# One-hot products with wide moving tokens, token tiles refilled when free, read-backs in turn, splits ahead of additions

## The chip, the cores and the metric

The kernel runs on one core of one Trainium2 chip. The metric is the device time of one execution in microseconds (us); times of the kernel before are the median of three runs. TensorE (PE) multiplies 128-row tiles, VectorE (DVE), ScalarE (ACT) and GpSimd (POOL) work on tiles of 128 partitions, SyncE (SP) issues most of the DMAs, and 16 DMA engines move the data between DRAM and the on-chip buffers. Each engine takes its instructions in the order in which the program holds them.

## The reference

512 tokens of 1024 values pass through one encoder layer: a norm, a mixer of a state-space branch and a latent attention, a cross-attention into 256 memory tokens, and a mixture of experts; everything in float32. The change lies in the mixture of experts, which is, for the 512 x 1024 matrix `t` of normed rows:

```python
g_idx = argmax(softmax(t @ w_group + b_group))            # one of 4 groups
top_v, top_i = top_k(e_logits of that group, 2)           # 2 of its 8 experts
gates = softmax(top_v) * max(g_prob), placed at the two experts, 0 elsewhere
for each of 32 experts e:
    out += (silu(t @ w_gate[e]) * (t @ w_up[e]) * gates[:, e]) @ w_down[e]
x = x + out;  result = rms(x) * norm_final_g
```

`w_gate` and `w_up` are 32 x 1024 x 256, `w_down` is 32 x 256 x 1024: 3 MB for each expert, 96 MB in all, and every expert's weights are read once.

## The kernel before

**The work before the experts.** Up to about 460 us of the span the kernel computes the mixer and the cross-attention. The last part of that, the output projection of the cross-attention (`pxo`), adds its result to the rows `X[t]`, t = 0 to 3, four tiles of 128 tokens. The four lie in two buffers (`xr`, two token tiles in each). The rows are written to two DRAM tables as they come: `hd`, from which they are gathered later, and `xd`, to which results are added.

**Routing.** For every token tile, `choose(t)` (L1385 on) takes the two experts on VectorE, and `place(t)` (L1423 on) has TensorE count, for each token and expert, how many tokens came before it (`prank`). A comparison of that rank with 64 slot numbers gives, for experts 0 and 1, a one-hot matrix `oh0[:, t]` of 128 tokens x 128 places (2 experts of 64 places). The experts are worked on in 16 pairs, with 64 places for each expert, so that a pair is a tile of 128 rows. `codes(t)` makes the one-hot tiles for the look-up of pairs 0 and 1, for three of the four token tiles on GpSimd and ScalarE, with `XG[1]` as the scratch. The list `OQ` (L64) is the written order of these steps: `00` is the one-hot product of token tile 0 and half 0, `P2` is `choose` and `place` of tile 2, `C0` is `codes(0)`.

**The first pair's rows.** Pair 0 isn't gathered: its rows are made by TensorE, straight in transposed form. `one_hot_T(g, c)` (L1439) takes, for half c of the 1024 values, four slices of 128 values of `X[t]` as weights (128 x 128) and the one-hot matrix (128 columns) as the moving operand, and sums over the four token tiles in a bank `px0[c]`. That is 4 x 2 x 4 = 32 products. `evac_T` (L1416) then multiplies a bank by the norm's gain into `XT`. All these products are tied in order to each other by `behind`, which fixes the order of issue without a wait.

**Look-up and gathers.** After the last one-hot product, `look_up` (L1591, `ptab0`) finds the token of each place, and `tokens` (L1602) writes the indices `IX`. With them GpSimd gathers the rows of pair n from `hd` into `XG[n % 2]` (L1694). Both `XG` tiles are first cleared, `XG[1]` at L1584 and `XG[0]` at L1699, because places without a token are skipped by a gather.

**The expert loop.** For pair n, `first(n)` transposes the gathered rows (`get`, L1764, eight transposes), multiplies by the gate and up weights (`pG`, L1784) and gates the result. `second(n)` (L1821 on) transposes it and multiplies by the down weights (`pD`, L1841). In pair 0, `get(1, 0)` stands between the first six and the last two slices of k. In iteration n, `second(n - 1)` follows `first(n)`. The results of pairs 0 to 13 are scattered into `xd` and `yd` (L1855), a token's first expert to one and its second to the other. Those of pairs 14 and 15 are split into a high and a low part (`split`, on ScalarE and VectorE) and are added at the end by products with a one-hot matrix (`last_sum`, L1915).

**The loads.** SyncE issues the expert weights in a fixed order, 96 tiles of 1 MB (`order`), into 24 buffers (`ring` and `tags`), most of which were used for other things earlier. `load_to(n)` (L1297) issues up to the n-th tile. A tile is issued when its buffer is free, and SyncE waits at a tile whose buffer isn't. The last two tiles of the first 24 (tag `X`, tiles 22 and 23) lie where `xr` was. For them alone (`after`, L1303) GpSimd writes a few zeros into the new tile, in an order behind the first gather, and the loads wait for that write. The call that reaches them, `load_to(ahead)`, is at L1700. Tiles 24 and 25 take the buffers of pair 0's first two weight tiles, 26 and 27 those of its other two.

**The end.** After the last scatter `take_back` (L1861) reads `yd` and then `xd` back, four reads of 512 KB each. VectorE's order at the end is written out by `turn_`. `both(t)` adds the two tables of token tile t. `down15` is the second half of pair 15 with its two splits, one for each half of the columns. Before, the order is split 0, `both(0)`, split 1, `both(1)`, `both(2)`, `both(3)`, then the additions of the sums (`a00` and on, the list `TO`). The rows of token tiles 2 and 3 are added on TensorE by products with the identity (L1909), those of tiles 0 and 1 by VectorE (L1924). Squares on ScalarE, a reciprocal and a product on VectorE and a store follow for each token tile and half.

## Time and profile before

| | |
|---|---|
| median of 3 runs | 732.78 us (732.72 to 732.96) |
| the profiled execution's own time | 733.54 us |
| its span, first to last instruction | 731.4 us |
| PE busy | 682.5 us (93%) |
| DVE busy | 416.3 us (57%) |
| ACT busy | 248.7 us (34%) |
| POOL busy | 113.8 us (16%) |
| chain that ended last | PE 52%, DMA 28%, DVE 13% of the span |
| granted TensorE clock, mean | 0.978 |

A row of a timeline gives the start in us from the first instruction of the span, the length, the engine, the line of the kernel, the operation, and output<-input. In brackets stands how long the engine was idle before it, and what ended that idle time. PEld is TensorE's load of weights, which runs beside its products. A product in float32 appears as two instructions, so the 32 one-hot products are 64 rows. A tile that is renamed in the source appears under the name of its first use: `px0` is shown as `pX`, the token tiles as `xr`. DMA share is the mean busy share of the 16 DMA engines.

### The profile page before, as it was taken

How to read it: one execution, taken by the hardware profiler on the slowest of the kernel's cores; microseconds unless marked ns; L12 is line 12 of the kernel's file. 1: busy time of each engine (PE TensorE's matmuls, PEld its weight loads, DVE VectorE, ACT ScalarE, POOL GpSimd, SP SyncE). 2: the span in 40 equal slices, each digit the busy share in tenths (PEclk: the TensorE clock that was granted, in tenths of full speed). 3: DMA queues.
4: the chain of work that ended last, by engine and by line, in shares of the span. 5: the costliest groups of instructions: out<-in, count | busy, mean ns of one | idle time of the engine just before them, and what ended most of it. 6: DMA issues, size and time to landing. Idle time of an engine off the chain costs nothing.

```text
span 731.4 us, 10262 instructions
## 1 busy us (share of the span) xinstructions
PE 682.5 (93%) x3684; PEld 469.9 (64%) x3684; DVE 416.3 (57%) x975; ACT 248.7 (34%) x511; POOL 113.8 (16%) x172
## 2 busy tenths in 40 slices
PE   5998988987999999999999999999998999998875
PEld 4696877975878887888878788963333333433333
DVE  4799997957477887555466543552533421221127
ACT  5642354344565766334345422221101000000023
POOL 6300002003300001102000001212332232232100
PEclk9999999999999999999999999999999999999996
DMA  7773132435452254232328896869999999999983
GB/s 213 168 206 109 38 74 67 114 123 127 145 164 68 92 153 131 99 84 84 107 80 339 271 338 240 282 251 390 409 408 408 410 404 410 407 413 388 397 337 121
DMA packets 102013, 165.84 MB, mean 227 GB/s; under 512 B 32762, under 2 KB 64606, under 8 KB 98120
## 3 DMA queue, kind: packets, MB, share of 16 engines
q1 hardware_dynamic: 95512, 157.58, 61.0%
q0 software_dynamic: 6432, 7.58, 3.1%
q8 instruction: 30, 0.49, 0.3%
q14 instruction: 23, 0.19, 0.1%
q10 hardware_dynamic: 16, 0.00, 0.0%
HBM read 154.59 MB, written 25.69 MB: 246 GB/s over the span
## 4 chain that ended last, share of the span: by engine, by line
PE 52%; DMA 28%; DVE 13%; ACT 2%; issue 2%; SPq 1%; POOL 0%; DVEq 0%; ACTq 0%
DMA gu<-moe_w_up 15%; DMA dn<-moe_w_down 6%; PE pG L1784 3%; DVE lo L214 2%; PE po L1034 2%; DMA raw<-w_in 2%; PE pX L1443 2%; PE pxq L268 2%; PE pxq L266 2%; PE pxq L267 2%; DMA gu<-moe_w_gate 2%; PE pD L1841 2%; PE pxo L266 2%; PE pPT L1023 2%; PE pxo L267 2%
## 5 line engine op out<-in xcount | busy, mean ns | idle before, releaser
L1784 PE MATMUL pG<-gu,XT 128*64 128x512 f32 x512 | 126.7, 595 | 5.3 <-DMA gu<-moe_w_up 5.2
L214 DVE TENSOR_TENSOR lo<-raw,hi 128x1024 fp32r<-128x1024 f32 (+3 forms) x64 | 75.9, 1190 | 60.5 <-ACT hi L204 60.1
L204 ACT ACTIVATE hi<-raw 128x1024 fp32r<-128x1024 f32 (+3 forms) x64 | 63.9, 1002 | 102.0 <-issue 21.1
L1784 PEld LDWEIGHTS pG<-gu,XT 128*64 128x64 f32 x512 | 40.4, 136 | 71.8 <-issue 68.5
L1841 PE MATMUL pD<-dn,aT 128*64 128x512 f32 x256 | 73.2, 601 | 1.8 <-DMA dn<-moe_w_down 1.8
L1807 DVE SCALAR_TENSOR_TENSOR a<-pG,RS,sl 128x256 f32<-128x256 f32 x16 | 10.7, 670 | 105.8 <-ACT sl L1801 65.4
L1801 ACT ACTIVATE sl<-pG,RS 128x256 f32<-128x256 f32 x16 | 7.6, 474 | 131.9 <-PE pG L1784 131.9
L1841 PEld LDWEIGHTS pD<-dn,aT 128*64 128x64 f32 x256 | 20.5, 136 | 36.4 <-issue 31.6
L1417 DVE TENSOR_TENSOR XT<-pX,gmo 128x512 f32<-128x512 f32 x32 | 22.0, 686 | 20.9 <-PE pX L1768 16.8
L1803 POOL TENSOR_SCALAR YY<-XG,F 128x1024 f32<-128x1024 f32 x13 | 15.2, 1169 | 107.1 <-issue 46.9
L1768 PEld LDWEIGHTS pX<-ident,XG 128*128 128x128 f32 x120 | 15.7, 194 | 25.0 <-issue 17.2
L1849 DVE SCALAR_TENSOR_TENSOR YY<-pD,GT,YY 128x512 f32<-128x512 f32 x26 | 19.5, 749 | 21.1 <-PE pD L1841 21.0
L1827 ACT ACTIVATE aT<-pA 128x256 f32<-128x256 f32 x16 | 6.1, 384 | 61.4 <-PE pD L1841 46.0
L1768 PE MATMUL pX<-ident,XG 128*128 128x128 f32 x120 | 21.0, 298 | 5.3 <-DMA XG<-hd,IX 5.2
L267 PE MATMUL pxq<-gT,hi 128*128 128x512 f32 x64 | 25.6, 400 | 0.0
L266 PE MATMUL pxq<-gT,hi 128*128 128x512 f32 x64 | 25.5, 399 | 0.0
L268 PE MATMUL pxq<-gT,lo 128*128 128x512 f32 x64 | 25.4, 396 | 0.0
L266 PE MATMUL pcq<-hT,hi 128*128 128x512 f32 x48 | 20.0, 416 | 2.8 <-DVE s_t L593 2.8
L267 PE MATMUL pq<-lo,cq 128*128 128x384 f32 x48 | 18.1, 376 | 2.3 <-DVE lo L214 2.3
L268 PE MATMUL pcq<-hT,lo 128*128 128x512 f32 x48 | 19.7, 410 | 0.0
L267 PE MATMUL pcq<-hT,hi 128*128 128x512 f32 x48 | 19.5, 407 | 0.0
L1855 POOL DMA_INDIRECT xd<-YY,IY x14 | 14.7, 1047 | 30.7 <-DVE YY L1849 25.7
(617 smaller groups left out, 1690.0 us busy)
## 6 DMA issues: line engine op xcount, KB each, us to landing
gu<-moe_w_gate SPq DMA_DIRECT2D x64, 512.0 KB
gu<-moe_w_up SPq DMA_DIRECT2D x64, 512.0 KB
dn<-moe_w_down SPq DMA_DIRECT2D x30, 1024.0 KB
raw<-w_in SPq DMA_DIRECT2D x9, 512.0 KB
raw<-xattn_w_v SPq DMA_DIRECT2D x8, 512.0 KB
raw<-xattn_w_k SPq DMA_DIRECT2D x8, 512.0 KB
raw<-w_out SPq DMA_DIRECT2D x8, 512.0 KB
raw<-xattn_w_q SPq DMA_DIRECT2D x8, 512.0 KB
```

What stands on the lines that cost most here:

```text
L204: anchor["act"] = nc.scalar.activation(hi, r, AF.Copy)
L214: anchor["dve"] = nc.vector.tensor_tensor(lo, r, hi.bitcast(F32), OP.subtract)
L266: i = nc.tensor.matmul(o, lh, rh, start=start, stop=False)
L267: nc.tensor.matmul(o, lh, rl, start=False, stop=False)
L268: anchor["pe"] = nc.tensor.matmul(o, ll, rh, start=False, stop=stop)
L1417: return v.tensor_tensor(xt, ps.rearrange("p (k t) -> p k t", k=4), gmo[:, 4 * c:4 * c + 4, None].to_broadcast([128, 4, 128]), OP.mult)
L1768: i = nc.tensor.transpose(ps[:, k * 128:k * 128 + 128], xg[:, 4 * c + k], ident)
L1784: i = nc.tensor.matmul(pg[64 * s:64 * s + 64], xt[c][:, kk, 64 * s:64 * s + 64], ew[2 * n + s, c][:, :, kk], start=k == 0, stop=k == 7)
L1803: nc.gpsimd.tensor_scalar(result(n), XG[n % 2], F1[:, n:n + 1], 1.0, OP.mult, OP.mult)
L1841: i = nc.tensor.matmul(pd[64 * s:64 * s + 64], at_[:, f, 64 * s:64 * s + 64], ew[2 * n + s, 2][:, f, c * 512:c * 512 + 512], start=f == 0, ...
L1849: yield v.scalar_tensor_tensor(o, pd, GT[:, n:n + 1], o, OP.mult, OP.add)
L1855: nc.gpsimd.indirect_dma_start(out=o, out_offset=bass.IndirectOffsetOnAxis(ap=IY[:, w, n:n + 1], axis=0), in_=Y, in_offset=None, bounds_ch ...
```

## The change

Four things are altered.

1. `one_hot_T` becomes `one_hot`: the one-hot matrix is the weight operand and 512 values of the token rows move, in one product for a token tile and a half, 8 in all. The rows come out untransposed. Two copies, one on ScalarE and one on VectorE, bring them into `XG[0]`, TensorE transposes them in eight steps and `evac_T` follows as before. The clearing of `XG[0]` goes. The token look-up keeps its place behind all of this in TensorE's order.
2. The loads of tiles 22 and 23 lose GpSimd's write and with it their place behind the first gather.
3. `take_back` reads `yd` and `xd` of one token tile after each other, into one buffer.
4. Both splits of pair 15 come ahead of all `both` additions. Besides, the transposes of pair n are put behind the last `pD` product of pair n - 2 in TensorE's order.

```diff
-            after = nheld + 1 + NF < nld[0] <= ahead
...
-                if after:
-                    behind(nc.gpsimd.memset(t[0:1, :, 0, 0:1], 0.0), gat[-1])
...
-    def one_hot_T(g, c):
+    def one_hot(g, c):
 
         for t in range(GR[g].start, GR[g].stop):
-            for k in range(4):
-                i = nc.tensor.matmul(px0[c][:, k * 128:k * 128 + 128],
-                                     X[t].rearrange("t (p k) -> t k p", k=8)[:, 4 * c + k],
-                                     oh0[:, t].rearrange("p e s -> p (e s)"), start=t == 0 and k == 0,
-                                     stop=t == NT - 1 and k == 3)
-                behind(i, last[0])
-                last[0] = i
+            i = nc.tensor.matmul(px0[c], oh0[:, t].rearrange("p e s -> p (e s)"), X[t][:, c * 512:c * 512 + 512],
+                                 start=t == 0, stop=t == NT - 1)
+            behind(i, last[0])
+            last[0] = i
...
-            one_hot_T(g, c)
-            if g == len(GR) - 1:
-                evac_T(xt0[c], px0[c], c)
-    gz = nc.gpsimd.memset(XG[1], 0.0)
+            one_hot(g, c)
+    nc.scalar.activation(XG[0][:, 0:512], px0[0], AF.Copy)
+    nc.vector.tensor_copy(XG[0][:, 512:D], px0[1])
+    for c in range(2):
+        ps = bankt(f"pXt0{c}")
+        for k in range(4):
+            i = nc.tensor.transpose(ps[:, k * 128:k * 128 + 128],
+                                    XG[0].rearrange("t (p k) -> t k p", k=8)[:, 4 * c + k], ident)
+            behind(i, last[0])
+            last[0] = i
+        evac_T(xt0[c], ps, c)
+    nc.gpsimd.memset(XG[1], 0.0)
...
-    nc.gpsimd.memset(XG[0], 0.0)
...
             behind(i, last[0])
+            behind(i, lastd.get(n - 2))
...
+            lastd[n] = i
...
-        for src, dst in ((yd, back), (xd, X)):
-            for t in range(NT):
-                if t % 2 == 0:
-                    xb = slot(next(free), [128, 2, D], f"xb{t}")
-                nc.sync.dma_start(xb[:, t % 2], src[128 * t:128 * t + 128])
-                dst[t] = xb[:, t % 2]
+        for t in range(NT):
+            xb = slot(next(free), [128, 2, D], f"xb{t}")
+            for i, (src, dst) in enumerate(((yd, back), (xd, X))):
+                nc.sync.dma_start(xb[:, i], src[128 * t:128 * t + 128])
+                dst[t] = xb[:, i]
...
-    for t, i in enumerate(down15):
+    for i in down15:
         turn_("v", i)
-        both(t)
-    for t in on_pe:
+    for t in range(NT):
         both(t)
```

## Rows read from the trace of the kernel before

**Rows 1.** The page, part 2: what the DMA engines moved in each fortieth of the span (18.3 us each), in GB/s.

```profile
GB/s 213 168 206 109 38 74 67 114 123 127 145 164 68 92 153 131 99 84 84 107 80 339 271 338 240 282 251 390 409 408 408 410 404 410 407 413 388 397 337 121
```

**Rows 2.** The chain of work that ended last, in order of time, from 530 us: start, length, and what ran or was waited for.

```profile
530.02 14.48 DMA gu<-moe_w_gate
...
699.36 1.93 PE pD L1841 x6
701.51 9.72 DMA xb<-xd
...
713.29 4.63 PE pC L1915 x10
717.93 2.52 PE pC L1909 x4
...
721.38 1.72 PE pC L1909 x4
```

**Rows 3.** Busy time by stretch (all engines): length, PE, PEld, DVE, ACT, POOL busy with their counts, granted clock, DMA share, GB/s.

```profile
480.00:485.00 5.00, 4.86 (x35) 3.35 (x34) 2.82 (x6) 0.00 (x0) 1.18 (x2) 1.00 0.14 57
485.00:490.00 5.00, 4.74 (x37) 1.69 (x34) 4.16 (x36) 1.62 (x4) 1.83 (x4) 1.00 0.67 229
490.00:495.00 5.00, 5.00 (x26) 2.13 (x26) 2.98 (x6) 0.64 (x2) 0.00 (x0) 1.00 1.00 310
495.00:500.00 5.00, 5.00 (x26) 1.60 (x24) 0.00 (x0) 0.00 (x0) 0.00 (x0) 1.00 0.99 382
...
550.00:600.00 50.00, 45.74 (x224) 17.12 (x221) 18.49 (x51) 3.51 (x10) 14.81 (x14) 1.00 1.02 406
```

**Rows 4.** The SyncE queue's waits between 460 and 500 us: waiting line, what it waited for, total, times, longest.

```profile
SPq L1308 <- POOL gu L1307: 14.9, 1, 14.9
```

**Rows 5.** Timeline of 480 to 500 us, the DMA issues only: the first gather by GpSimd and the loads that SyncE issues after it.

```profile
484.36 1.35 POOL L1694 DMA_INDIRECT XG<-hd,IX  x1 [3.82 <-DVE IX L1605]
...
485.83 0.33 SPq L1308 DMA_DIRECT2D gu<-moe_w_gate  x1
...
487.87 0.39 SPq L1308 DMA_DIRECT2D gu<-moe_w_gate  x1
...
492.99 0.91 SPq L1323 DMA_DIRECT2D dn<-moe_w_down  x2
```

**Rows 6.** The chain again, 465 to 493 us: the pieces of the one-hot products (L1443), and of the second pair's transposes (L1768) and the first pair's last products (L1784).

```profile
465.54 1.02 PE pX L1443 x4
...
467.00 1.91 PE pX L1443 x8
...
469.73 2.93 PE pX L1443 x12
472.72 3.90 PE pX L1443 x16
476.71 5.82 PE pX L1443 x24
...
490.46 0.64 PE pX L1768 x4
491.10 1.87 PE pG L1784 x8
```

**Rows 7.** Timeline of 463 to 480 us: the routing of the last token tile (its logits, the places of the tile before, its own places), ScalarE's code operations and the clearing that follows them.

```profile
469.83 0.25 DVE L1391 SCALAR_TENSOR_TENSOR r_lg<-plog,st_moe,br 128x36 f32<-128x36 f32 x1 [2.39 <-PE plog L1362]
...
472.77 0.29 DVE L1435 TENSOR_TENSOR oh<-prank,slots 128x128 f32<-128x128 f32 x1 [1.28 <-PE prank L1430]
...
476.76 0.29 DVE L1435 TENSOR_TENSOR oh<-prank,slots 128x128 f32<-128x128 f32 x1 [1.57 <-PE prank L1430]
...
477.18 0.71 ACT L1562 ACTIVATE XG<-XG 128x256 f32<-128x256 f32 x2
...
479.59 0.95 POOL L1584 MEMSET XG<- 128x1024 f32 x1 [4.72 <-ACT ohb L1563]
```

**Rows 8.** Timeline of 480 to 500 us: an evacuation of transposed rows, the token look-up, the first expert product, the token indices.

```profile
480.65 0.69 DVE L1417 TENSOR_TENSOR XT<-pX,gmo 128x512 f32<-128x512 f32 x1 [2.91 <-PE pX L1443]
...
482.35 0.34 PE L1595 MATMUL ptab<-vals,ohb 128*128 128x2 bf16 x8
...
482.63 1.93 PE L1784 MATMUL pG<-gu,XT 128*64 128x512 f32 x6
...
483.35 0.17 DVE L1605 TENSOR_SCALAR IX<-TK 128x2 int32<-128x2 f32 x1
```

**Rows 9.** The gathered tile XG: time from issue to landing of its 15 gathers.

```profile
DMA to landing us min/median/max: 7.0/8.4/8.9
```

**Rows 10.** Timeline of the last 47 us: ScalarE's half of the last split, the additions of the read-back tables, the additions of the sums, the last squares.

```profile
707.01 0.69 ACT L276 ACTIVATE Y<-pD,GT 128x512 fp32r<-128x512 f32 x1 [1.03 <-PE pD L1841]
711.35 1.23 DVE L1939 TENSOR_TENSOR xb<-xb,xb 128x1024 f32<-128x1024 f32 x1 [4.58 <-DMA xb<-xd]
...
713.15 3.49 DVE L1939 TENSOR_TENSOR xb<-xb,xb 128x1024 f32<-128x1024 f32 x3
...
716.56 2.47 DVE L1924 TENSOR_TENSOR xb<-xb,pC 128x512 f32<-128x512 f32 x4
...
723.59 0.60 ACT L329 ACTIVATE fin<-pC 128x512 f32<-128x512 f32 x1 [0.82 <-PE pC L1915]
```

**Rows 11.** Busy time by stretch near the end (columns as in rows 3).

```profile
714.00:715.00 1.00, 1.00 (x4) 0.81 (x3) 1.00 (x2) 0.00 (x0) 0.00 (x0) 0.50 0.06 25
```

More of the change, by code (lines that the diff above doesn't have):

```diff
@@ L1311, in load_to @@
                 t = slot(tag, [128, 2, D], f"dn{e}")
-                if after:
-                    behind(nc.gpsimd.memset(t[0:1, 0, 0:1], 0.0), gat[-1])
                 if i == 94:
@@ L1751, in overflow @@
                     nc.sync.dma_start(out[0, t * 128:t * 128 + 128, half[c]], o[:, t])
-    silu, YY = [None], []
+    silu, YY, lastd = [None], [], {}
     turns = {}
```

## The prediction

> **What bounds the kernel now.** I read the page's bandwidth line first: from about 494 us to 696 us the DMA engines move close to 410 GB/s, and before that they don't [rows 1]. The chain of waits says the same from its side: from 530 us on it consists of weight loads, up to the last down products at 699.36, and then of the read-back of the tables and the closing sums [rows 2]. So the second half is a stream of weights at full rate, and its end is set by when the stream was first able to run without a gap. The stretches show the gap: the share is 0.14 between 480 and 485 us and 0.67 between 485 and 490, and 0.99 to 1.02 afterwards [rows 3]. That is 0.86 x 5 + 0.33 x 5 = 5.95 us in which the engines stood still, and every such microsecond comes back at the end of the stream. The SyncE queue says why: one wait of 14.9 us on GpSimd's write at L1307 [rows 4]. The write stands behind the first gather at 484.36, and the held load goes out at 485.83 [rows 5].
>
> **The one-hot products.** In the chain the old ones take 1.02 + 1.91 + 2.93 + 3.90 + 5.82 = 15.58 us for 64 rows [rows 6]. The new ones are 8 products of 512 float32 columns, 16 rows. No such row with a one-hot weight exists, but the identity products at L1909 have the same shape: 1.72 / 4 = 0.43 us a row in the last piece, 2.52 / 4 = 0.63 in the first, which ran partly at the lower clock [rows 2]. I take 16 x 0.43 = 6.9 us (bounds 3.7, if a row took the 0.23 of the old ones, and 10.1). The eight transposes cost 2 x 0.64 = 1.28 us [rows 6]. TensorE thus has 7.4 us less to do, but it will wait for the routing, so I follow the chain.
>
> The last tile's routing began at 469.83 on VectorE, after 12 of the one-hot rows [rows 6, 7]. Of those about four of the wide rows remain (1.7 instead of 2.93 us), so it begins near 468.6. From there to its one-hot matrix took 469.83 to 477.05, of which 1.28 was a wait for ranks that stood behind one-hot products [rows 7]; without that 5.9 us, so the matrix is there at 474.5. The two products that need it take 4 x 0.43: 476.2. VectorE's copy of a bank is priced by an evacuation of the same size, 0.69 us [rows 8]: 476.9. ScalarE's copy comes later, because its code operations began 0.13 us behind the one-hot matrix and took until 479.59 [rows 7], 2.4 us: here to 477.0, and with 0.69 to 477.7. Both banks are needed by every transpose, because a slice takes every eighth value. The transposes end at 479.0, the first four at 478.4, and the first evacuation (0.69) at 479.1. The look-up needs the bank that this frees, so it starts at 479.1 instead of 482.35, and the expert products at 479.2 instead of 482.63; the indices follow the look-up by 1.0, at 480.1 instead of 483.35, and the gather starts at 484.36 - 3.25 = 481.1 [rows 5, 8]. So half of the 7.4 us is lost to waiting, and TensorE is about 3.4 us earlier (bounds 0 and 6).
>
> **The refilled buffers.** Tiles 22 and 23 now wait only for the last reader of `xr`, near 476, while the DMA engines are busy until about 480.6 (5 - 0.86 x 5 = 0.7 us of work after 480 [rows 3]). They hold 2.1 MB, 5.1 us at the 406 to 410 GB/s of the stream: work until 485.8. Tiles 24 and 25 went out at 487.87, 5.24 us after the first expert product [rows 5, 8]; now at 484.5, in time, and give work to 490.9. Two gathers of at most 0.5 MB each add up to 2.6 us; I count 1.2, since many places are empty: 492.1. Tiles 26 and 27 need the end of pair 0, which stands behind the first gather. A gather lands 7.0 to 8.9 us after its issue, median 8.4 [rows 9]; from 481.1 that is 489.5, then a transpose group and the last products, 0.64 + 1.87 [rows 6]: 492.0, with half a microsecond until bytes move. So a gap of 0 to 1.4 us stays; I take 0.8. The stream gains 5.95 - 0.8 = 5.15 us, say 5.2. Upper end 7.1: no gap, and the slow stretch of 490 to 495 (310 instead of 406 GB/s, 1.2 us [rows 3]) gone as well. Lower end 3.2: TensorE no earlier, a gap of 2.1 and a start of 0.6 before tile 24. The cleared tile and GpSimd's writes were beside other work and give nothing; the order of the transposes behind `pD` costs TensorE under 1 us a pair, hidden, since the loads and not TensorE set the pace of the loop from 530 us on.
>
> **The end.** In the trace ScalarE has its half of the last split ready at 707.70, but VectorE stands at the first `both` until 711.35, waiting for a read-back; only then comes the split, and TensorE starts again at 713.29 [rows 2, 10]. It restarts at half its clock: granted 0.50, that is 1.2 of 2.4 GHz, around 714.5, after an idle time of nearly 3 us [rows 11]. In the changed order the split ends near 708.5 and TensorE goes on without that pause. The additions `both` then start as each token tile's two reads have landed. When the eighth read lands isn't shown; it lies between 711.35 (the fifth awaited one) and 715.5, where the last of the three additions of 713.15 ran without a wait (713.15 + 2 x 1.16) [rows 10]. The sums' additions, at 716.56 before, start between 713.8 and 716.7; I take 715.5, so 1.1 earlier. ScalarE's wait of 0.82 for TensorE before the last squares [rows 10] goes too, if the clock stays up. Together 1.9 us, between 0.2 (reads as late as before, TensorE at half clock again) and 3.6 (2.8 + 0.82).
>
> What the fifth read shows is that it took 9.72 us from its issue, nearly as long as all eight took to move [rows 2]. The Trainium skill (DMA: Bandwidth & Descriptors, "Queues, rings and completion order") states that each DMA engine consumes its ring's descriptors in order. By that the eighth read would land three reads after the fifth, 711.35 + 3 x 1.28 = 715.2, and the end would gain about 1.0 instead of 1.9; 9.72 us for the fifth of eight speaks rather for a share among all. No run here shows which.
>
> **The sum.** 5.2 + 1.9 = 7.1 us. The profiled execution took 733.54 us, 2.14 more than its span, and lies 0.76 above the median; that difference I leave alone. 733.54 - 7.1 = 726.4, and for the median 732.78 - 7.1 = 725.7.
>
> **Rivals.**
> A. *The front gains nothing.* The routing chain on VectorE, the copies and the transposes eat all that the short products give, and pair 0 starts as before. For it speaks that 5.9 of the 7.2 us of that chain are VectorE's own [rows 7]; against it the 7.4 us taken from TensorE. Tile 24 then goes out at 487.87 with the engines idle since 485.8: stream 3.2, sum 5.1, 727.7 us.
> B. *The read-backs come as late as before*, and TensorE falls to half clock once more. Stream 5.2, end 0.2, sum 5.4: 727.4 us.
> C. *The change doesn't do what it says:* the two loads find another holder of their buffers and go out only with the gather. The gap then moves forward with the gather alone, 3.25 us: sum 5.2, 727.6 us.
> D. *Slower: the gather starves behind the loads.* The loads that are no longer held share the DMA engines with the first gather, whose rows stand in the middle of pair 0, in front of everything on TensorE; and pair 0's end frees tiles 26 and 27. Every microsecond that the gather lands after 489.5 is a microsecond of idle DMA. The whole gain is used up when it lands at 489.5 + 7.1 = 496.6, which is 15.5 us after its issue. At twice the slowest, 17.8 us, it lands at 498.9: idle 0.8 + 9.4 = 10.2 instead of 5.95, a loss of 4.3, less 1.9: 735.2 us. Against it: most of the 15 gathers ran within the full stream, and none took over 8.9 us [rows 9].
> E. *No difference:* two of A to C together and a gap behind 492 as long as the old one, within 1.5 us of 732.8.
>
> **How the numbers follow.** Forecast 0.60, A 0.13, B 0.12, C 0.05, D 0.06, E 0.04. The likeliest is 725.7, so that is the prediction. The ends of the terms give 3.2 + 0.2 = 3.4 and 7.1 + 3.6 = 10.7 us, thus 722.1 to 729.4; I take 722.2 to 729.6, which holds A to C and leaves out D and E. A measurement of this kernel can tell about 0.2%, 1.5 us, from no change. Faster by more than that: forecast and A to C, 0.90; within: 0.04; slower: 0.06.
>
> **What would show each step right or wrong.** The profile of the changed kernel should show 16 rows of 0.43 us for the one-hot products and eight transposes behind them; no SyncE wait on GpSimd, and loads going out near 472 to 476; a DMA share near 1 from 480 to 492, with at most a short dip after; the first expert product near 479 and the gather near 481, landing before 490; the last down load some 5 us earlier; and, from there on, VectorE's split ahead of the first `both` with no TensorE pause of 3 us. The prediction is wrong if the DMA share dips for more than 2 us around 485 to 495, if the expert products start no earlier than 482, or if the sums' additions come as long after the last down load as before.

## The result and the profile after

The changed kernel takes 723.95 us (median of 4 runs, 721.77 to 726.70), the kernel before 732.75 (4 runs, 732.33 to 732.96): ratio 0.9883, 95% interval 0.9848 to 0.9917, 8.8 us faster. The forecast was 725.7, its range 722.2 to 729.6. The profiled execution took 723.57 us with a span of 721.8; before it was 733.54 and 731.4.

Where the time went is seen first in the stretches that [rows 3] showed. Changed kernel, busy time by stretch (columns as there, the last three are granted clock, DMA share, GB/s):

```profile
475.00:480.00 5.00, 3.80 (x33) 2.07 (x34) 3.42 (x7) 2.15 (x6) 1.80 (x2) 1.00 1.03 426
480.00:485.00 5.00, 4.62 (x34) 1.61 (x34) 4.27 (x36) 1.58 (x4) 1.48 (x2) 1.00 1.00 404
485.00:490.00 5.00, 3.60 (x18) 1.53 (x16) 1.74 (x4) 0.68 (x2) 0.00 (x0) 1.00 1.02 401
490.00:495.00 5.00, 5.00 (x25) 1.78 (x26) 1.27 (x2) 0.00 (x0) 0.00 (x0) 1.00 1.05 423
495.00:500.00 5.00, 4.53 (x30) 1.55 (x28) 2.21 (x10) 0.91 (x3) 2.20 (x2) 1.00 1.00 410
```

The share of 0.14 and 0.67 is now 1.00 and 1.02, and the 310 and 382 GB/s of the next two stretches are 423 and 410. No stretch from 475 us on has a gap. The queue that held the loads back, SyncE's, waits no more for GpSimd. In place of the 14.9 us of [rows 4] it waits for the one-hot products, 3.5 us at the longest, which the first of these two views shows, and longer than before for the products of pair 0 whose buffers it refills (8.9 and 5.3 us at the lines of the two kinds of load, before 2.9 and 2.7). The second view shows when the loads went out:

```profile
SPq L1305 <- PE pX L1437: 4.6, 2, 3.5
```

```profile
471.31 0.80 SPq L1305 DMA_DIRECT2D gu<-moe_w_gate  x2
...
475.22 0.33 SPq L1305 DMA_DIRECT2D gu<-moe_w_gate  x1
...
481.88 0.33 SPq L1305 DMA_DIRECT2D gu<-moe_w_gate  x1
...
483.10 0.38 SPq L1305 DMA_DIRECT2D gu<-moe_w_gate  x1
...
489.47 0.80 SPq L1318 DMA_DIRECT2D dn<-moe_w_down  x2
```

These are tile 22 (471.31, with the gate half of the tile behind it), 23, 24, 25 and the two down tiles 26 and 27. Before, the held load went out at 485.83, tile 24 at 487.87 and tile 26 at 492.99 [rows 5].

The front, from the timeline of the changed kernel: the last tile's one-hot matrix, the two copies of the banks, the new transposes, the first expert product, the indices, the first gather.

```profile
472.52 0.29 DVE L1430 TENSOR_TENSOR oh<-prank,slots 128x128 f32<-128x128 f32 x1 [0.27 <-PE prank L1425]
...
474.33 0.60 ACT L1574 ACTIVATE XG<-pX 128x512 f32<-128x512 f32 x1 [1.29 <-PE pX L1437]
...
475.19 0.69 DVE L1575 COPY XG<-pX 128x512 f32<-128x512 f32 x1 [1.69 <-PE pX L1437]
...
476.03 1.13 PE L1579 MATMUL pXt<-ident,XG 128*128 128x128 f32 x8 [0.88 <-ACT ohb L1555]
...
477.76 1.93 PE L1784 MATMUL pG<-gu,XT 128*64 128x512 f32 x6
...
478.14 0.17 DVE L1605 TENSOR_SCALAR IX<-TK 128x2 int32<-128x2 f32 x1
...
479.15 1.34 POOL L1694 DMA_INDIRECT XG<-hd,IX  x1 [0.96 <-DMA gu<-moe_w_up]
```

The chain that ended last now runs through that gather (start, length, what):

```profile
472.49 1.83 PE pX L1437 x4
...
479.15 7.61 DMA XG<-hd,IX
...
489.44 0.64 PE pX L1767 x4
```

And the end, from the timeline: the product on the last down load, the last read-back's issue, the first products behind the splits, the last split, the four additions of the tables with TensorE's restart among them, the additions of the sums:

```profile
691.37 1.93 PE L1841 MATMUL pD<-dn,aT 128*64 128x512 f32 x6 [1.49 <-DMA dn<-moe_w_down]
...
696.72 0.32 SPq L1867 DMA_DIRECT2D xb<-xd  x1
...
698.91 5.84 PE L1915 MATMUL pC<-Y,oht 128*128 128x512 f32 x24
699.75 0.75 DVE L277 SCALAR_TENSOR_TENSOR Y<-pD,GT,Y 128x512 fp32r<-128x512 f32 x1 [0.97 <-ACT Y L276]
...
700.41 1.22 DVE L1939 TENSOR_TENSOR xb<-xb 128x1024 f32<-128x1024 f32 x1
701.88 1.23 DVE L1939 TENSOR_TENSOR xb<-xb 128x1024 f32<-128x1024 f32 x1 [0.25 <-DMA xb<-xd]
704.34 1.23 DVE L1939 TENSOR_TENSOR xb<-xb 128x1024 f32<-128x1024 f32 x1 [1.23 <-DMA xb<-xd]
...
705.62 1.98 PE L1909 MATMUL pC<-xb,ident 128*128 128x512 f32 x4 [0.87 <-DVE xb L1939]
706.95 1.23 DVE L1939 TENSOR_TENSOR xb<-xb 128x1024 f32<-128x1024 f32 x1 [1.39 <-DMA xb<-xd]
...
708.09 2.47 DVE L1924 TENSOR_TENSOR xb<-xb,pC 128x512 f32<-128x512 f32 x4
```

The split no longer stands behind an addition, and of TensorE's pause of 2.87 us in the kernel before 0.87 is left. But the last three additions each wait for a read-back, 2.46 and 2.61 us apart, and the sums follow the last one. Counted from the product on the last down load, the sums' additions start after 16.72 us (before 716.56 - 699.36 = 17.20 [rows 2, 10]) and the span ends after 30.43 (before 32.04). From the sums' additions to the end it is thus 13.71 us, where before had 14.84. So of the 9.6 us of the two spans, about 1.6 come from the end and 8 from what lies ahead of the last down load.

### The profile page after: what moved, and what is told of

The parts are those of the page before. It is cut to its first block, busy times and chain, and to the rows that moved or that the text cites. A ratio compares the mean times of both kernels' runs of the same rounds, so it can differ in the third digit from the quotient of the medians.

```text
span 721.8 us, 10176 instructions
## 1 busy us (share of the span) xinstructions
PE 672.7 (93%) x3644; PEld 474.8 (66%) x3644; DVE 415.1 (58%) x976; ACT 249.3 (35%) x512; POOL 112.5 (16%) x169
## 4 chain that ended last, share of the span: by engine, by line
PE 47%; DMA 31%; DVE 13%; ACT 4%; issue 2%; SPq 1%; POOL 1%; DVEq 0%; ACTq 0%
DMA gu<-moe_w_up 19%; DMA dn<-moe_w_down 7%; PE po L1034 2%; DVE lo L214 2%; PE pxq L266 2%; PE pxq L267 2%; PE pxq L268 2%; PE pG L1784 2%; PE pxo L266 2%; DMA raw<-w_in 2%; PE pPT L1023 2%; PE pxo L267 2%; PE pxo L268 1%; DMA xb<-xd 1%; DMA XG<-hd,IX 1%
## 5 line engine op out<-in xcount | busy, mean ns | idle before, releaser
L1784 PE MATMUL pG<-gu,XT 128*64 128x512 f32 x512 | 117.9, 595 | 5.9 <-DMA gu<-moe_w_up 2.3
L1784 PEld LDWEIGHTS pG<-gu,XT 128*64 128x64 f32 x512 | 53.6, 137 | 56.8 <-issue 50.3
L1841 PE MATMUL pD<-dn,aT 128*64 128x512 f32 x256 | 71.1, 599 | 2.0 <-DMA dn<-moe_w_down 1.5
L1841 PEld LDWEIGHTS pD<-dn,aT 128*64 128x64 f32 x256 | 22.1, 136 | 37.5 <-issue 33.8
L1412 DVE TENSOR_TENSOR XT<-pX,gmo 128x512 f32<-128x512 f32 x30 | 19.3, 682 | 7.1 <-PE pX L1767 7.1
L266 PE MATMUL pcq<-hT,hi 128*128 128x512 f32 x48 | 19.3, 402 | 2.9 <-DVE s_t L593 2.9
L1767 PE MATMUL pX<-ident,XG 128*128 128x128 f32 x120 | 17.6, 288 | 3.5 <-DMA XG<-hd,IX 3.5
L1018 ACT ACTIVATE P<-psc,sm 128x128 f32<-128x128 f32 (+3 forms) x32 | 16.8, 528 | 7.2 <-DVE sm L1017 7.1
```

The costliest lines, as they stand in the source:

```text
L266: i = nc.tensor.matmul(o, lh, rh, start=start, stop=False)
L1018: nc.scalar.activation(P[:, 0:nk], ps[:, 0:nk], AF.Exp, bias=st[:, 0:1], accum_out=st[:, 1:2])
L1412: return v.tensor_tensor(xt, ps.rearrange("p (k t) -> p k t", k=4), gmo[:, 4 * c:4 * c + 4, None].to_broadcast([128, 4, 128]), OP.mult)
L1767: i = nc.tensor.transpose(ps[:, k * 128:k * 128 + 128], xg[:, 4 * c + k], ident)
L1784: i = nc.tensor.matmul(pg[64 * s:64 * s + 64], xt[c][:, kk, 64 * s:64 * s + 64], ew[2 * n + s, c][:, :, kk], start=k == 0, stop=k == 7)
L1841: i = nc.tensor.matmul(pd[64 * s:64 * s + 64], at_[:, f, 64 * s:64 * s + 64], ew[2 * n + s, 2][:, f, c * 512:c * 512 + 512], start=f == 0, ...
```

## The experiments

Theory: the gain is the closed gap of the DMA engines; the shorter one-hot products and the released loads each close a part of it, and the end gives about a microsecond. Rivals: the end's order carries a good part; the released loads cost the gather what they bring; one of the two front parts does it all. The kernels below were timed in five rounds beside the kernel before, in three sets, which gave that one 733.31 (729.88 to 734.69), 733.03 (730.41 to 734.70) and 732.92 us (729.91 to 734.22). Single runs of one kernel thus scatter by some 4 us, so each kernel's trace is used beside its ratio. This table is worked out from the traces. S: from the first one-hot product to TensorE's product on the last down load. E: from there to the end of the span. MB: what the DMA engines moved from 465 to 505 us. Idle: one minus their share, summed over the same 40 us in steps of 1 us, where a share above 1 counts as 1. The unchanged part ahead of it is not equally long in every execution: the first one-hot product starts between 463.57 us (v_end) and 468.30 (v_order). Counted over 40 us from that product, MB changes by 0.12 at most.

```
                        ratio to before            S       E      MB     idle
before                                           233.99  32.04  12.21   7.14
changed                 0.9883 [0.9848, 0.9917]  225.45  30.43  15.43   0.99
again (changed)         0.9903 [0.9877, 0.9928]  227.59  30.44  15.16   1.16
u12      old front      0.9990 [0.9974, 1.0006]  233.39  30.70  12.22   6.90
u34      old end        0.9895 [0.9872, 0.9918]  226.13  30.87  15.35   0.96
b1       products only  0.9915 [0.9896, 0.9934]  227.76  31.06  14.26   1.80
u2       old hold       0.9907 [0.9886, 0.9928]  227.47  30.45  14.55   1.49
b2       no hold only   0.9965 [0.9947, 0.9983]  228.91  32.28  13.46   4.54
u1       old products   0.9931 [0.9910, 0.9953]  230.12  30.49  13.67   3.65
v_order                 0.9888 [0.9866, 0.9910]  225.82  30.98  15.37   0.88
v_end                   0.9886 [0.9866, 0.9906]  225.60  30.03  15.44   0.89
v_end2                  0.9884 [0.9858, 0.9911]  225.82  29.90  15.24   1.03
```

**The changed kernel once more**, unchanged, beside the next four.

> The changed kernel once more, as the control for the three others. If its runs spread over several microseconds again, that spread belongs to this kernel or to the granted clock in the unchanged first half, and single times can't be compared below that; if the clock in the first 260 us explains it, the length from the first read-back to the end stays at 31.4 us and the DMA share stays at 1.00 or above from 475 to 500 us, whatever the total is.

Measured: 725.3 us (723.51 to 728.22), 8.0 below before. S is 2.1 us longer than in the first profile with nearly the same bytes in the gap's place (15.16 against 15.43 MB), so a single trace's S is good to about 2 us, its MB to about 0.3.

**The front undone (u12)**: the old one-hot products and the hold by GpSimd are back, the end and the order of the transposes stay changed.

```diff
-            i = nc.tensor.matmul(px0[c], oh0[:, t]..., X[t][:, c * 512:c * 512 + 512], ...)
+            for k in range(4):
+                i = nc.tensor.matmul(px0[c][:, k * 128:k * 128 + 128], X[t]...[:, 4 * c + k], oh0[:, t]..., ...)
...
+            after = nheld + 1 + NF < nld[0] <= ahead
+                if after:
+                    behind(nc.gpsimd.memset(t[0:1, :, 0, 0:1], 0.0), gat[-1])
```

> The changed kernel with the old one-hot products and GpSimd's write back, so only the end (read-backs in turn, splits ahead) and the order of the transposes are changed. By the forecast's account of the end 1.9 us below the kernel before; by the account that the reads land in the order of issue 0.4 to 1.2 us below it. The gap of about 6 us around 480 to 487 us is there in full.

Measured: 732.51 us (728.96 to 734.42), no difference to before that can be told. The gap is back in full (6.9 us idle, 12.22 MB), SyncE's wait for GpSimd too. E is 1.3 us shorter than before. So the front carries the gain, and the end's part is too small to be seen in the time. The old products bring the clearing of `XG[0]` back with them, so all that follows on the products holds for the two together.

**The end undone (u34)**: read-backs of the one table, then of the other, and splits between the additions, as before.

```diff
-        for t in range(NT):
-            xb = slot(next(free), [128, 2, D], f"xb{t}")
-            for i, (src, dst) in enumerate(((yd, back), (xd, X))):
+        for src, dst in ((yd, back), (xd, X)):
+            for t in range(NT):
...
-    for i in down15:
-        turn_("v", i)
+    for t, i in enumerate(down15):
+        turn_("v", i)
+        both(t)
```

> The changed kernel with the read-backs in the old order and the old order of splits and additions, so both parts of the end undone. Forecast's account: 1.9 us lost again, TensorE pauses for about 3 us and falls to half clock. Rival (the reads land in the order of issue and the last one sets the additions, so the end gains little): 0.4 to 1 us lost; first read-back to end 31.4 us in the changed kernel becomes about 31.8, as before the change.

Measured: 725.01 us (723.59 to 726.82), as the changed kernel. TensorE pauses again, but the timeline and the stretches show what the pause is worth:

```profile
707.08 2.58 PE L1916 MATMUL pC<-Y,oht 128*128 128x512 f32 x10 [2.69 <-DVE Y L277]
```

```profile
706.00:708.00 2.00, 0.92 (x4) 0.79 (x5) 2.00 (x3) 0.00 (x0) 0.00 (x0) 1.00 0.23 92
708.00:710.00 2.00, 2.00 (x10) 1.42 (x9) 2.00 (x3) 0.00 (x0) 0.00 (x0) 1.00 0.05 20
```

After 2.69 us of idle it goes on at a granted clock of 1.00, not at the 0.50 of [rows 11]; and the additions of the sums start 17.01 us after the product on the last down load, 0.3 later than in the changed kernel. Over the six rows of the table with the changed end (the v_end pair apart) E is 30.58 us in the mean (30.43 to 30.98), over the four with the old one 31.56 (30.87 to 32.28): about 1.0 us.

These four aren't alike, though, and what divides them is TensorE's clock. In the kernel before and in b2 (an experiment below) the ten products behind the pause ran at 0.50 and took 4.63 [rows 2] and 4.64 us, in u34 2.58. First b2, then u34, the restart and the additions of the sums:

```profile
710.36 4.64 PE L1911 MATMUL pC<-Y,oht 128*128 128x512 f32 x10 [3.04 <-DVE Y L277]
713.62 2.48 DVE L1920 TENSOR_TENSOR xb<-xb,pC 128x512 f32<-128x512 f32 x4
```

```profile
710.34 2.47 DVE L1925 TENSOR_TENSOR xb<-xb,pC 128x512 f32<-128x512 f32 x4
```

From the additions of the sums to the end it takes 14.84 us in the kernel before and 14.78 in b2, but 13.86 in u34 and 13.71 in b1, as in the six with the changed end (13.68 to 13.77). Ahead of the additions of the sums the old end takes 17.27 us in the mean (17.01 to 17.50), the changed one 16.85 (16.69 to 17.30). So the order itself is worth about 0.4 us, and another 1.1 us are lost where TensorE runs the closing products at half clock. ScalarE's wait of 0.82 us [rows 10] goes with the clock too: b2 has it, u34 doesn't.

**The new products alone (b1)**: the kernel before with the changed one-hot products, copies and transposes and without the clearing of `XG[0]`, the rest as before (the lines of the diff from `one_hot_T` to the clearing).

> The kernel before with the new one-hot products alone: the hold, the old end and the old order of the transposes stay. Theory (the hold costs little once the gather itself is early): the gather issues near 479, the gap shrinks from 6 us to about 1, and the time is 5 to 7 us below the kernel before. Rival (only both parts together close the gap): 3 us or less below.

Measured: 726.85 us (723.97 to 727.36). The wait of SyncE for GpSimd is still there, but 9.7 us long, because the gather in front of it goes out at 479.62 instead of 484.36:

```profile
SPq L1308 <- POOL gu L1307: 9.7, 1, 9.7
```

```profile
480.00:485.00 5.00, 4.87 (x42) 1.98 (x42) 3.80 (x36) 1.35 (x4) 2.09 (x4) 1.00 0.91 303
485.00:490.00 5.00, 5.00 (x24) 2.01 (x24) 3.05 (x7) 0.90 (x2) 0.00 (x0) 1.00 0.92 310
```

Between 475 and 490 us 0.95 us of idle time are left of 6.04. The one part thus does most of the work, and also on the part that it was not written for: the earlier gather ends the hold earlier.

**The hold kept beside the new products and the new end (u2)**: the lines with `after` and `behind(nc.gpsimd.memset...)` as in u12.

> The changed kernel with GpSimd's write before tiles 22 and 23 back, so that they wait for the first gather's issue. Theory: the gather now goes out near 479.2 and ends its issue near 480.5, just where the engines run out of other loads, so the gap that comes back is only 0.5 to 2 us and the time rises by as much; the gather lands sooner than 7.6 us after its issue. Rival (the hold alone made the old gap): a gap of 5 to 6 us and the time 5 to 6 us higher.

Measured: 725.48 us (724.91 to 726.71), as "again" to within 0.2 us; the 0.5 to 2 us that were expected to be lost don't show, and S is that of "again" too (227.47 and 227.59). MB and idle time are near those of b1 (14.55 MB, 1.49 us idle). The gather found the DMA engines nearly free here: it went out at 478.40, and TensorE's first transposes of its rows ran at 484.44, 6.04 us later and without a wait.

**The hold removed alone (b2)**: the kernel before without the lines that u12 puts back.

> The kernel before with one part of the change alone: GpSimd no longer holds tiles 22 and 23 back (one-hot products, read-backs and splits as before). Theory (the two front parts close the same gap, each most of it by itself): the SyncE queue shows no wait on GpSimd but a stand of about 7 us at tile 22, the DMA engines stand still for about 3 us around 470 to 475 and hardly at all from 475 to 490, the span from the first one-hot product to the first read-back is 228 to 229.5 us (before 234.3), and the time is about 5 us below before: 728 (727 to 729). Rival (the parts add up, the one-hot part brought 6.2 of the 8 us, so 1 to 2 are left for this one): 731 to 732, with a first part of 232 us or more and a share well below 1 after 480.

Measured: 730.36 us (726.84 to 731.94), 2.6 below before, between the theory's 728 and the rival's 731 to 732. SyncE's queue stands as the theory said, 7.7 us. The idle time is somewhat larger and later than the theory had it: 1.31 us from 465 to 475 and 2.71 from 475 to 490, most of it ahead of 480. S is 5.1 us shorter than before, more than the times say; the first one-hot product of this execution started 1.84 us later than before's. The wait and the two stretches:

```profile
SPq L1305 <- PE pX L1438: 12.5, 2, 7.7
```

```profile
470.00:475.00 5.00, 5.00 (x30) 4.99 (x29) 1.87 (x11) 0.07 (x1) 0.00 (x0) 1.00 0.82 274
475.00:480.00 5.00, 5.00 (x26) 4.99 (x25) 2.65 (x6) 1.21 (x5) 1.50 (x2) 1.00 0.48 152
```

With the old products `xr` is read until about 476 us, tile 22 waits for that, and the three tiles behind it on the queue, whose buffers are free, wait with it.

**The old products beside the rest of the change (u1)**.

> The changed kernel with the old one-hot products, everything else as changed. Theory (idle DMA engines set the end): tile 23 waits for the last one-hot product near 482.5 and tiles 24 and 25 for the first expert products near 488, while the engines run out at about 485.8; a gap of 2 to 3 us comes back, so the time is 2 to 4 us above the changed kernel's. Rival (TensorE's work sets the end): the 7.4 us of products come back in full, 6 to 8 us. Second rival (the refilled buffers alone do it): within 1 us of the changed kernel.

Measured: 727.99 us (725.55 to 730.75), the size that was expected and not the place: the dip isn't behind 485 but between 470 and 475, from the same stand of the queue as in b2.

```profile
470.00:475.00 5.00, 5.00 (x25) 4.99 (x25) 2.85 (x9) 0.20 (x1) 1.50 (x2) 1.00 0.48 178
```

Do the two front parts add up? In bytes moved by 505 us, the new products alone bring 14.26 - 12.21 = 2.05 (b1) and 14.55 - 12.22 = 2.33 MB (u2 against u12), the removed hold alone 1.25 (b2) and 1.45 (u1 against u12), both together 2.9 to 3.2. At 406 GB/s a megabyte is 2.46 us: 5.0 to 5.7 us, 3.1 to 3.6 us, and 7.2 to 7.9 us. So they nearly add up; the same 0.4 to 2.1 us are closed by either. In the times (ratios, times 733) it is 6.1 to 6.2, 2.6 to 4.3 and 6.4 to 7.8. That removing the hold is still worth 1.5 to 2.7 us once the products are short (15.16 and 15.43 against 14.55 MB, 15.35 against 14.26) is argued from the bytes alone and not shown, since u2 and "again" can't be told apart in time or in S.

**The order of the transposes undone (u5)**.

```diff
-            behind(i, lastd.get(n - 2))
```

> The changed kernel without the order of the transposes behind the down products of two pairs earlier. Theory (the order is hidden, the loads set the pace): 725 us, within 1 us of the unchanged kernel of the earlier calls, first one-hot product to first read-back 224 to 227 us, stream at 405 to 407 GB/s. Rival (without the order the transposes run ahead of the down products, buffers come free later and the stream thins): 727 or more, and a DMA share below 0.97 in some windows from 500 to 680.

Measured: 725.72 us (722.99 to 726.58), ratio 0.9904 [0.9880, 0.9928], as the changed kernel; the engines move 408 GB/s from 500 to 680 us, and from the first one-hot product to the end it takes 256.30 us (changed: 255.88). The order is hidden. (It has no row in the table, since TensorE reached the last down load without waiting for it.)

**Tiles 22 and 23 behind the three tiles whose buffers are free (v_order)**, to fill the dip that is left at the head of the queue.

```diff
+                ds = [nc.sync.dma_start(t[:, 0], ...), nc.sync.dma_start(t[:, 1], ...)]
+                for d in ds:
+                    for p in sent[-3:] if after else ():
+                        behind(d, p)
```

> The changed kernel with the loads of tiles 22 and 23 kept behind the three tiles before them on SyncE (in the changed kernel the first load of tile 22 was issued ahead of three tiles whose buffers were free, and SyncE stood 3.5 us at it). Theory: the dip of the DMA share to about 0.8 between 470 and 475 goes and the time falls by 0.5 to 1 us, less than the spread of the runs; the length from the first one-hot product to the first read-back falls below 226 us. Rival (the dip is filled later anyway): no difference.

Measured: 724.75 us (721.21 to 727.0); a share of 0.88 stays between 470 and 475, where the idle time of the changed kernel (0.82 us from 465 to 475) is that of before anyway, and S is that of the changed kernel. This brought nothing that can be measured; what the dip then waits for wasn't followed up.

**The read-backs in the order in which they are needed (v_end, v_end2)**: token tiles 2 and 3 first, whose sums go through TensorE; the additions of tiles 0 and 1 later. v_end2 also moves the scaling of tile 2 behind the sums of tile 1.

```diff
-        for t in range(NT):
+        for t in (2, 3, 0, 1):
...
-            for i, (src, dst) in enumerate(((yd, back), (xd, X))):
+            for i, (src, dst) in enumerate(((xd, X), (yd, back))):
...
-TO = 'a00 s00 a01 s01 a10 s10 a11 s11 o00 o01 s20 s21 o10 o11 s30 s31 o20 o21 o30 o31'.split()
+TO = 's20 s21 b0 a00 s00 a01 s01 o20 o21 b1 s30 s31 a10 s10 a11 s11 o00 o01 o30 o31 o10 o11'.split()
```

> The changed kernel with another end: the read-backs of token tiles 2 and 3 first, and the additions of tiles 0 and 1 after the squares of tiles 2 and 3 have begun. Theory (reads land in the order of issue, 1.28 us apart, and the last one held up everything behind it): the squares on ScalarE begin 3 to 4 us sooner after the first read-back and the end comes 1.5 to 3 us sooner. Rival (the reads share the DMA engines and all land near the last): no gain, or a loss, since the same landing now stands in front of TensorE's identity products.

> The changed kernel with the read-backs of token tiles 2 and 3 first and their table xd ahead of yd, the additions of tiles 0 and 1 behind them, and the scaling of tile 2 behind the sums of tile 1 (in the earlier version of this order the scaling of tile 2 stood 1.12 us for the ninth transfer and held the addition of tile 1 up by 3.9 us). Theory (VectorE's chain behind the last read-back sets the end): the addition of tile 1 starts 17.4 us after the first read-back's issue instead of 20.0, the end comes 30.0 to 30.7 us after that issue (31.6 in the earlier version, 31.4 in the changed kernel), about 724 us. Rival (the last read-back lands too late for it): the addition of tile 1 waits for its transfer until 19 us or later, the end at 31.4, and the time as the changed kernel's, 725.

Measured: 723.86 (720.96 to 725.37) and 723.46 us (722.25 to 726.28), 1.4 and 1.8 below "again", whose runs they overlap. E is 30.03 and 29.90 us, 0.4 to 0.5 shorter than in the changed kernel, where 1.5 to 3 had been expected of the first of the two. In v_end the scaling of tile 2 waited for the ninth transfer, and the addition of tile 1 stood behind it:

```profile
706.31 1.41 DVE L1935 SCALAR_TENSOR_TENSOR xg<-pC,st_fin,fin 128x512 f32<-128x512 f32 x2 [1.12 <-DMA fin<-norm_final_g]
707.63 1.22 DVE L1939 TENSOR_TENSOR xb<-xb 128x1024 f32<-128x1024 f32 x1
```

In v_end2 that wait is gone, and TensorE's sums are late in its place:

```profile
707.06 1.28 DVE L1924 TENSOR_TENSOR xb<-xb,pC 128x512 f32<-128x512 f32 x2 [0.52 <-PE pC L1915]
708.26 1.22 DVE L1939 TENSOR_TENSOR xb<-xb 128x1024 f32<-128x1024 f32 x1
...
710.62 1.28 DVE L1924 TENSOR_TENSOR xb<-xb,pC 128x512 f32<-128x512 f32 x2 [1.15 <-PE pC L1915]
```

Its first read-back goes out at 688.22, but the second only at 691.11, so its addition of tile 1 at 708.26 comes 20.0 us after the first issue, as the rival said, though no transfer holds that addition up. Three orders of the end, and E moves by half a microsecond: in all nine profiles with the reads in turn, the additions that wait for a read start 2.4 to 2.6 us apart, and behind the last of them stands VectorE's closing chain. These two are the fastest medians of the study; that they beat the changed kernel isn't shown.

## Why the prediction was right

**The bound and the mechanism held.** A stream of weights whose end is set by a gap of 5.95 us [rows 3]: the gap is closed, the last down load's product comes 8 us earlier, and u12, which brings the gap back, brings the time back. The size was less well met: the stream gave more than the upper end of its own term and the end less than forecast, and that the two misses partly cancel is luck.

**The stream's term was too small: 5.2 forecast (3.2 to 7.1), 7.9 from the bytes** (3.2 MB at 406 GB/s). The upper end had been worked out as no gap at all plus the slow stretch of 490 to 495 gone, and that is what happened: idle from 475 to 490 us fell from 6.04 to 0.07, and the stretches behind it run at 423 and 410 GB/s. That the gain is still 0.8 above the upper end lies in counting idle time and not bytes: in [rows 3] the stretch of 485 to 490 has a share of 0.67 but moves only 229 GB/s. Against 406 GB/s the four stretches of 480 to 500 lack 4.3, 2.2, 1.2 and 0.3 us, 8.0 together. The step that failed is the gap of 0.8 us forecast behind 492.1. Tiles 26 and 27 went out at 489.47, not at 492.5.

**Why they were earlier: the front.** The first expert product was forecast at 479.2 and came at 477.76, 4.9 us earlier than before where 3.4 had been taken.
- The start of the last tile's routing was forecast at 468.6 and came at 469.39, 0.8 too late; 0.55 of that is that the first one-hot product came so much later in this execution (465.92 against 465.37).
- From there to its one-hot matrix I took 7.22 - 1.28 = 5.9 us; it took 472.81 - 469.39 = 3.42. [Rows 7] had shown two waits for ranks, 1.28 and 1.57, both behind one-hot products, and I took out one. Of the second 0.27 is left. The third piece stood in no row of mine: one operation of the routing on VectorE took 1.44 us before and 0.24 now. 1.28 + 1.30 + 1.20 = 3.78, which is the difference but for 0.02. Before, GpSimd's clearing of `XG[0]` ran beside that operation and ended 0.04 us ahead of it; the third row is the operation in the changed kernel, which has no clearing there:

```profile
473.47 1.44 DVE L1401 TENSOR_SCALAR r_o<-f_code,r_i 128x32 f32<-128x32 f32 x1
473.92 0.95 POOL L1699 MEMSET XG<- 128x1024 f32 x1
```

```profile
471.73 0.24 DVE L1396 TENSOR_SCALAR r_o<-f_code,r_i 128x32 f32<-128x32 f32 x1
```

All four kernels with that clearing (before, u12, b2, u1) show 1.44, the others 0.24. So the forecast that the clearing was "beside other work" and gives nothing is the step that missed this piece. No run takes the clearing out alone.
- The products took what the identity products had priced, 0.43 to 0.46 us a row (1.83 us for the last four on the chain).
- ScalarE's copy was forecast at 477.0, behind its code operations. It ran at 474.33, ahead of them, and the transposes then waited 0.88 us, by the profile for one of ScalarE's code operations; VectorE's copy, which they need as well, ended at 475.88, 0.15 before they began. The first evacuation was done at 477.44 (476.75 + 0.69), not at 479.1.

**The gather** was forecast at 481.1, 8.4 us to landing. It went out at 479.15, and the chain has 7.61 us for it. TensorE waited 1.40 us for it; pair 0's end came at 489.44, 2.6 earlier than forecast.

**Loads.** Tiles 22 and 23 at 471.31 and 475.22 (forecast 472 to 476), 24 and 25 at 481.88 and 483.10 (forecast 484.5). What the forecast lacked is the queue: tile 22 now stands at the head of SyncE's for 3.5 us, with loads behind it that could have gone. In b2 and u1, where the products are old, this costs 2.7 to 3.6 us of idle time more than in the changed kernel.

**The end was too large: 1.9 forecast (0.2 to 3.6), 1.6 between the two profiles, about 1.0 as the mean over ten.** The step that failed is the landing of the reads. From the fifth read's 9.72 us [rows 2] I concluded that the eight share the engines and that the sums' additions start 1.1 us earlier; they start 0.5 earlier (16.72 against 17.20; 0.4 over the ten profiles). By its own sign of being wrong, sums as long after the last down load as before, the term only just held. The reads land one after the other: the additions of tiles 1, 2 and 3, each waiting for its second read, started at 701.88, 704.34 and 706.95, so about 1.27 us a read, in the order of issue. This agrees with what the Trainium skill (DMA: Bandwidth & Descriptors, "Queues, rings and completion order") states of a ring, that each engine consumes its descriptors in order. The forecast's estimate by it (1.0 in all, without ScalarE's 0.82 some 0.2 for the sums) lies nearer to the 0.4 to 0.5 than 1.1 does. Nor were the 9.72 us a share: the additions that waited for the fourth, sixth and eighth read started 10.13, 10.31 and 10.23 us after these were issued (691.75, 694.03 and 696.72). Some ten microseconds stood ahead of a read wherever it was in the order, which looks like the length of the line. The last read also came late for the DMA engines: their mean share was 0.68, 0.39, 0.23 and 0.12 in the four microseconds from 703 to 707. What held its last bytes back wasn't followed up.

The other part of the end, ScalarE's wait of 0.82 us ahead of the last squares, is gone as forecast (they start at 714.11 and 714.92 with no idle time named), and for the reason that the forecast gave: the clock stayed up. It was worth 14.84 - 13.71 = 1.13 us, since u34, with the old order and a clock of 1.00, needs 13.86. But the old order doesn't lose this each time. Of its four profiles two ran the closing products at 0.50 and lost it, the two others needed 13.86 and 13.71, so the gain of 1.6 us between the two profiles holds some 0.5 us of the order and 1.1 of the clock in the profile of before.

**The rivals.** A fell with 477.76; B is refuted as to its pause and its clock, though its remainder, reads that come no sooner, was nearly right (0.4 to 0.5 us); C fell with the view of SyncE's waits. D, the gather that starves, has a true core: with the hold kept TensorE used its rows 6.04 us after the issue, with the loads beside it 7.74 us. As TensorE didn't wait for them at 6.04, they may have landed earlier still; the price is at least 1.7 us of gather and 1.4 us of TensorE waiting. It is 7.74 us in all, far from the 15.5 that would have made it slower.

## What to carry to other kernels

Where a stream of loads sets the end, look for the place where it first stands still and count bytes there, not idle time alone: a busy share of 0.67 hid a rate of little more than half. The megabytes moved by a fixed point set the kernels with one part apart from those with both, where six runs of each couldn't always; but they are a reading of the gap, not of the time, as u2 and "again" show. When loads are released from one wait, look at what they then wait for at the head of their queue, and at what stands behind them: with the long products some 12 us of the hold's 15 came back as two waits for them, and loads whose buffers were free stood behind the longer one (7.3 to 7.7 us). And reads that were queued together landed one after the other, about 1.3 us apart, so their order decided which came first, and hardly when the last one came.

## What the runs showed of the hardware

- A gather beside a full stream took 7.6 us on the chain; with the DMA engines partly free its rows were in use after 6.04.
- TensorE's granted clock behind the pause of the old end: 1.00 after 2.69 us (u34); 0.50 after 2.87 (before, until 719) and after 3.04 (b2, until 716); 1.00 at first after 3.02 and then 0.50 from about 710 to 713 (b1). With the changed end (the v_end pair apart), where the pause is 0.87 to 1.97 us, it was 1.00 through the closing products in every profile. No run here varies the pause alone, so what decides isn't shown.
- One operation of 128 x 32 elements on VectorE took 1.44 us in the four kernels in which GpSimd's clearing of a 128 x 1024 tile ran beside it, and 0.24 us in the others. The same operation for the token tile before took 0.50 to 0.51 in every kernel, beside two GpSimd operations on 128 x 256 elements. No run takes a GpSimd operation out alone.
- The first 215 us, which no kernel here changes, ran at clocks that differ from execution to execution: from 50 to 70 us 0.91 in the profile of before, 1.00 in the first of the changed kernel and 0.83 in the second. The first one-hot product started at 463.57 us in the fastest of the profiles (v_end), where the mean clock of those 215 us was 0.97, and at 468.30 in the latest (v_order, 0.94).
